# Low parts of every second weight tile of the second feed-forward product: from a VectorE subtraction to an adding DMA

## The chip, the cores and the metric

One Trainium2 chip; the kernel runs on one of its NeuronCores. The metric is the device time of one execution in microseconds (us), as the median of several runs. Engines are named as in the profile: PE (TensorE, its weight loads apart as PEld), DVE (VectorE), ACT (ScalarE), POOL (GpSimd) and SP (SyncE, which here only issues DMAs).

## What is computed

Two residual layers over 512 tokens of width 1024, and a final norm. Each layer has a token mixer (a state-space branch, a sparse attention, a retention, merged by gates) and a feed-forward part. The change lies in the feed-forward part, whose reference is:

```python
h2 = rms_norm(x, norm2_g[l])
x = x + jnp.square(jax.nn.relu(h2 @ w_ff1[l])) @ w_ff2[l]
```

`w_ff1` is 1024 x 4096 and `w_ff2` 4096 x 1024, in float32.

## The kernel before, in words

**Products in three passes.** Every large product keeps float32 accuracy by splitting both factors into a head (`wh`, `sqh`, ... of type float32r) and a low part (`wl`, `sql`, ...). `mm3` (L256) adds three matmuls into one PSUM bank: head by head, low part of the activation by the head of the weight, and head of the activation by the low part of the weight. So the low part of a weight tile is needed by one matmul in three.

**Weight tiles.** `wload` (L225) makes one tile of 128 partitions by up to 1024 floats (512 KB): SP issues a DMA from HBM into `raw`, ACT copies `raw` to the head `wh`, and DVE subtracts, `wl = raw - wh` (L233). Each of the three has three buffers, shared by all weight tiles of the kernel, those of `wload7` too. A buffer of `raw` is free for the next load when nobody has to read it any more; before, that is when the subtraction is done. A buffer of `wh` and `wl` is free when the last matmul on it is done.

**The feed-forward stage.** `layer` walks over 8 groups of 512 hidden features. For each group and each `part` (0, 1), it calls `ff1` for a piece of the next group, and then `ff2(e, part)` (L1194). `ff1` multiplies by a seven-product scheme: four tiles from `wload7` (128 x 896, DVE builds three of their blocks out of the others by additions in `raw`), 21 matmuls of 256 columns on each, into four PSUM banks named `f7` (the profile calls them `f`), and then DVE and ACT square and split the result (`zz`, `sqh`, `sql`). `ff2` calls `fm_blocks` (L261) for four blocks of 128 output features, two at a time: `b0` = 0 and `b0` = 2. Each pair needs one tile of `w_ff2`, 128 x 1024, with 24 matmuls of 512 columns on it, and DVE adds the two PSUM banks (`mm`) to the residual `xp`. So one `ff1` and one `ff2` are six weight tiles: four of 84 matmuls together, and two of 24 each. The last group of the second layer goes another way (256 columns at a time) and is not touched by the change. While layer 0 is in this stage, DVE, ACT and POOL also prepare the state-space tables of layer 1 (`s5_prep`).

**What sets the order.** Each engine runs its instructions in order. The order is found at build time by the framework's scheduler, which works on its own estimates; weight tiles are called under `high_priority` (look-ahead 3000), so that their copies and subtractions are pulled ahead as far as the buffers allow. All weight loads are in one line on SP.

Of the kernel before, what the change touches and what calls it, by code (L numbers as in the profile page):

```python
# [13 lines left out]
ALU = mybir.AluOpType  # L14

P = 128
SEQ = 512
# [76 lines left out]
def build(tc, x, positions, norm1_g, w_in, lam_re, lam_im, log_step, b_re, b_im, c_re, c_im, ssm_d,  # L94
# [26 lines left out]
    pe, ve, sc, gp, sy = (Ordered(e) for e in (nc.tensor, nc.vector, nc.scalar, nc.gpsimd, nc.sync))  # L121
    es = contextlib.ExitStack()
    with es:
# [4 lines left out]
        def f(t):  # L128
            return t.bitcast(F32)
# [9 lines left out]
        def spage(dtype=F32, name="tb"):  # L139
            return page(dtype, name, "tb")  # L140
# [13 lines left out]
        def copy(o, i, scale=1.0):  # L154
            sc.activation(o, i, AF.Copy, scale=scale)
# [66 lines left out]

        LOOK = 3000

        def wload(src, a, n, look=LOOK):  # L225
            with tc.high_priority(look):
                raw = pool.tile([P, 1024], F32, tag="raw", bufs=3, name="raw")
                h = pool.tile([P, 1024], F32R, tag="wh", bufs=3, name="wh")
                lo = pool.tile([P, 1024], F32R, tag="wl", bufs=3, name="wl")
                rv, hv, lv = (z[:, :a * n].rearrange("p (a n) -> p a n", a=a) for z in (raw, h, lo))  # L230
                sy.dma_start(out=rv, in_=src.rearrange("(k p) n -> p k n", p=P))
                copy(h[:, :a * n], raw[:, :a * n])
                ve.tensor_tensor(lo[:, :a * n], raw[:, :a * n], f(h[:, :a * n]), ALU.subtract)  # L233
            return hv, lv

        def wload7(src, look=LOOK):
# [17 lines left out]
        def mm3(ps, sh, sl, mh, ml, first, last, after=None):  # L254
            r = pe.matmul(ps, sh, mh, start=first, stop=False)
            if after is not None:  # L256
                tc.add_manual_dep(r.ins, after, order, reason="held back")
            pe.matmul(ps, sh, ml, start=False, stop=False)
            pe.matmul(ps, sl, mh, start=False, stop=last)

        def fm_blocks(w, c0, nblk, xh, xl, psf, n=SEQ, look=LOOK, after=None):  # L261
            kb = len(xh)
            step = 4 if kb == 2 else 2
            kp = min(kb, 4)
            for b0 in range(0, nblk, step):
                ps = [None] * step
                for k0 in range(0, kb, kp):
                    wh, wl = wload(w[k0 * P:(k0 + kp) * P, c0 + b0 * P:c0 + (b0 + step) * P], kp, step * P, look)
                    for j in range(step):
                        if k0 == 0:  # L270
                            ps[j] = psf()
                        cc = slice(j * P, (j + 1) * P)
                        for k in range(kp):
                            mm3(ps[j][:, :n], wh[:, k, cc], wl[:, k, cc], xh[k0 + k], xl[k0 + k], k0 + k == 0, k0 + k == kb - 1, after)
                        after = None
                for j in range(step):
                    yield b0 + j, ps[j]
# [419 lines left out]
        def s5_glu(l, gf, res):  # L697
            gh, gl = [], []
            for g in gf:
                h, lo = spage(F32R, "s5h"), spage(F32R, "s5l")  # L700
                copy(h, g)
                lo_of(lo, g, h)
                gh.append(h)
                gl.append(lo)
            wh, wl = wload(glu_w[l], 2, 256)
            for m in range(2):
                ps = mx_ps("glu")
                for k in range(2):
                    mm3(ps, wh[:, k, m * P:(m + 1) * P], wl[:, k, m * P:(m + 1) * P], gh[k], gl[k], k == 0, k == 1)
                th = spage(name="s5q")  # L710
                sc.activation(th, ps, AF.Tanh, scale=0.25, bias=glb2[:, 2 * l + m:2 * l + m + 1])
                stt(th, th, 1.0, gf[m], ALU.add, ALU.mult)
                h, lo = page(F32R, "yah"), page(F32R, "yal")
                copy(h, th, 0.25)
                stt(lo, th, 0.25, f(h), ALU.mult, ALU.subtract)
                res.append((h, lo))


        def tm_group(l, c0, n, nrm, psf):
            pss = [psf() for _ in range(NT)]  # L720
            for kk in range(0, KB, 2):
                wp = wload(w_in[l][kk * P:(kk + 2) * P, c0:c0 + n], 2, n)
                for k in range(kk, kk + 2):
                    wh, wl = wp[0][:, k - kk], wp[1][:, k - kk]
                    for t in range(NT):
                        c = slice(t * P, (t + 1) * P)
                        mm3(pss[t][:, :n], nrm.h[k][:, c], nrm.l[k][:, c], wh, wl, k == 0, k == KB - 1)
            return pss

        def tr4(blocks, psf=None):  # L730

            ps = (psf or mx_ps)("tr")
            for t, b in enumerate(blocks):
                w = b.shape[-1]
                pe.transpose(ps[:w, t * P:(t + 1) * P], b, ident)
            return ps
# [307 lines left out]
        def proj(w, y, psf):  # L1044
            return fm_blocks(w, 0, KB, [a for a, _ in y], [b for _, b in y], psf, look=50)

        def layer(l, nrm, o5):
# [7 lines left out]
            def gates(br, b0, b1, pages, after=None):  # L1055
                return {b0 + b: gate_tile(ps, rb, pages)
                        for b, ps in fm_blocks(w_in[l], C_GATE + br * DM + b0 * P, b1 - b0, nrm.h, nrm.l, mm_ps, look=50, after=after)}
# [6 lines left out]
            def fill():  # L1064
                for b, ps in fm_blocks(w_in[l], C_GATE, KB, nrm.h, nrm.l, mm_ps, look=50):
                    acc[b] = gate_tile(ps, rb)
                return gates(2, 0, 2, gpage)
# [126 lines left out]
            def ff2(e, part):  # L1194
                hs, ls = sq[e]
                w2 = w_ff2[l][e * 512:(e + 1) * 512]
                if e < NE - 1 or l + 1 < DEPTH:
                    for m, ps in fm_blocks(w2, 4 * part * P, 4, hs, ls, mm_ps):
                        m += 4 * part
                        ve.tensor_tensor(xp[m], xp[m], ps, ALU.add)  # L1200
                        if e == NE - 1:
                            n3.feed(m, g1[:, (l + 1) * KB + m:(l + 1) * KB + m + 1])
                    return
                if part:
                    return
                fg = []
                for hf in range(2):
                    z = spage(name="fg")
                    sy.dma_start(out=z, in_=fin_g[hf * 512:(hf + 1) * 512].partition_broadcast(P))
                    fg.append(z)  # L1210
                for th in range(2):
                    cc = slice(256 * th, 256 * th + 256)
                    for m, ps in fm_blocks(w2, 0, KB, [q[:, cc] for q in hs], [q[:, cc] for q in ls], mm_ps, 256):
                        ve.tensor_tensor(xp[m][:, cc], xp[m][:, cc], ps[:, :256], ALU.add)
                        n3.feed(m, None, None, cc)
                    finish(n3, th, fg)

            def finish(n3, th, fg):
                ts = range(2 * th, 2 * th + 2)
                ot = {}  # L1220
                for hf in range(2):
                    for t in ts:
                        ps = tr4([xp[4 * hf + m][:, t * P:(t + 1) * P] for m in range(4)])
                        ot[t, hf] = spage(name="ot")
                        ve.tensor_tensor(ot[t, hf], ps, fg[hf], ALU.mult)
                r, _ = n3.stats(False, ts)
                for q, (t, hf) in enumerate((t, hf) for hf in range(2) for t in ts):
                    z = ot[t, hf]
                    if q % 2 == 1:
                        copy(z, z, r[:, t:t + 1])  # L1230
                    else:
                        ve.tensor_scalar(z, z, r[:, t:t + 1], None, op0=ALU.mult)
                    (sy if q % 2 == 0 else sc).dma_start(out=out[0, t * P:(t + 1) * P, hf * 512:(hf + 1) * 512], in_=z)
# [5 lines left out]
            for e in range(NE):  # L1239
                for part in range(2):  # L1240
                    if e + 1 < NE:
                        ff1(2 * e + 2 + part)
                    ff2(e, part)
                if e:
                    next(steps, None)
# [6 lines left out]
        for m in range(KB):  # L1252
            if m == 4:
                glb2 = more_consts()
            ps = tr4([xt[m // 4, t][:, (m % 4) * P:(m % 4 + 1) * P] for t in range(NT)])
# [28 lines left out]
```

## Time and profile before

| | us |
|---|---|
| median of 3 runs | 1519.19 (1518.92 to 1520.07) |
| profiled execution | 1518.57 |
| its span, first to last instruction | 1516.8 |
| PE busy | 1468.6 (97%) |
| DVE busy | 1224.0 (81%) |
| ACT busy | 696.2 (46%) |
| POOL busy | 59.3 (4%) |
| feed-forward stage, layer 0 | about 450 to 790 of the span |
| feed-forward stage, layer 1 | about 1190 to 1500 |

The page gives busy times, the share of 40 slices of the span, the chain of work that ended last, the costliest groups of instructions and the DMA issues. PE's busy time includes pipelined matmuls, so two matmuls overlap in it; the distance from start to start says how fast they follow each other.

### The profile page before, as it was taken

What the parts mean: (1) busy time and instruction counts of PE and PEld (TensorE: products, weight loads), DVE (VectorE), ACT (ScalarE), POOL (GpSimd) and SP (SyncE); (2) the same over time, 40 slices, a digit from 0 to 9 for tenths busy, and PEclk for the clock granted to TensorE, in tenths of its full rate; (3) what the DMA queues carried; (4) which work ended last, traced back from release to release, by engine and by line L of the source; (5) the groups of instructions that cost most, each with busy time, mean ns of one, the idle gap of its engine ahead of it and who ended that gap; (6) DMA issues with size and microseconds to landing.
All of it is one profiled execution on the core that took longest, in us unless ns stands there. A gap on an engine that the chain in (4) does not pass through costs nothing.

```text
span 1516.8 us, 22081 instructions
## 1 busy us (share of the span) xinstructions
PE 1468.6 (97%) x8202; PEld 1288.4 (85%) x8202; DVE 1224.0 (81%) x2618; ACT 696.2 (46%) x1154; POOL 59.3 (4%) x131
## 2 busy tenths in 40 slices
PE   5999999999998999999999999999999999999997
PEld 5888988877887998889888889988778888998887
DVE  7876899985899878987775769998568888777876
ACT  5654653453534443344455743344445434343343
POOL 0211100000010000100001100000000000000000
PEclk9899999999999999999999999999999999999999
DMA  6221222323322333233342223322143323333343
GB/s 221 77 81 42 81 70 73 94 70 101 108 63 91 111 98 99 83 108 95 119 130 76 84 57 94 94 70 84 56 153 90 95 93 98 111 98 102 94 126 111
DMA packets 138993, 144.17 MB, mean 95 GB/s; under 512 B 11835, under 2 KB 131461, under 8 KB 138885
## 3 DMA queue, kind: packets, MB, share of 16 engines
q1 hardware_dynamic: 138132, 141.63, 31.0%
q8 instruction: 64, 1.05, 0.3%
q10 hardware_dynamic: 752, 1.12, 0.2%
q14 instruction: 45, 0.36, 0.1%
HBM read 136.44 MB, written 6.29 MB: 94 GB/s over the span
## 4 chain that ended last, share of the span: by engine, by line
PE 83%; DVE 10%; ACT 4%; issue 2%; DMA 1%; POOL 0%; SPq 0%; POOLq 0%; DVEq 0%; ACTq 0%
PE mm L110 58%; PE f L110 17%; DVE wl L110 2%; ACT u L110 1%; PE mx L110 1%; PE pv L110 1%; PE sp L110 1%; PE ry L110 1%; PE tr L110 1%; DVE zr L110 1%; DVE ang L110 1%; PE pt L110 1%; ACT s5f L110 1%; DVE x L110 1%; PE s5y L110 1%
## 5 line engine op out<-in xcount | busy, mean ns | idle before, releaser
L110 ACT ACTIVATE wh<-raw 128x1024 fp32r<-128x1024 f32 (+4 forms) x318 | 310.4, 978 | 528.6 <-PE mm L110 287.7
L110 DVE TENSOR_TENSOR wl<-raw,wh 128x1024 fp32r<-128x1024 f32 (+4 forms) x318 | 355.2, 1118 | 120.0 <-ACT wh L110 116.7
L110 PE MATMUL f<-xc,wh 128*128 128x256 f32 x1344 | 242.8, 281 | 0.0
L110 PE MATMUL mm<-sql,wh 128*128 128x512 f32 (+1 forms) x544 | 207.2, 382 | 1.3 <-DVE sql L110 1.2
L110 PE MATMUL mm<-sqh,wh 128*128 128x512 f32 (+1 forms) x544 | 207.0, 382 | 1.3 <-DVE fft L110 1.1
L110 PE MATMUL mm<-sqh,wl 128*128 128x512 f32 (+1 forms) x544 | 206.1, 381 | 0.0
L110 PEld LDWEIGHTS f<-xc,wh 128*128 128x128 f32 x1344 | 205.4, 188 | 0.0
L110 PE MATMUL f<-xc,wl 128*128 128x256 f32 x644 | 174.6, 281 | 1.3 <-DVE wl L110 1.3
L110 PE MATMUL mm<-xgh,wh 128*128 128x512 f32 x384 | 152.3, 397 | 0.0
L110 PE MATMUL mm<-xgh,wl 128*128 128x512 f32 x384 | 152.1, 397 | 0.0
L110 PE MATMUL mm<-xgl,wh 128*128 128x512 f32 x384 | 151.9, 396 | 0.0
L110 DVE TENSOR_TENSOR raw<-raw 128x256 f32<-128x256 f32 (+1 forms) x336 | 107.3, 330 | 30.0 <-DMA raw<-in_w_ff_dram 27.8
L110 PEld LDWEIGHTS mm<-sql,wh 128*128 128x128 f32 x544 | 102.3, 188 | 21.6 <-DVE sql L110 1.9
L110 PEld LDWEIGHTS mm<-sqh,wh 128*128 128x128 f32 x544 | 102.2, 188 | 21.7 <-issue 1.5
L110 PEld LDWEIGHTS f<-xc,wl 128*128 128x128 f32 x644 | 118.7, 188 | 1.9 <-DVE wl L110 1.5
L110 PEld LDWEIGHTS mm<-sqh,wl 128*128 128x128 f32 x544 | 102.4, 188 | 21.0
L110 PE MATMUL mm<-wl,xgh 128*128 128x384 f32 (+1 forms) x320 | 107.5, 338 | 1.7 <-DVE wl L110 1.7
L110 PE MATMUL mm<-wh,xgh 128*128 128x384 f32 (+1 forms) x320 | 103.5, 340 | 4.6 <-ACT z L110 2.8
L110 PE MATMUL mm<-wh,xgl 128*128 128x384 f32 (+1 forms) x320 | 104.5, 338 | 0.0
L110 DVE TENSOR_TENSOR x<-x,mm 128x512 f32<-128x512 f32 (+1 forms) x136 | 88.3, 650 | 12.9 <-PE mm L110 12.6
L110 PEld LDWEIGHTS mm<-xgh,wl 128*128 128x128 f32 x384 | 72.3, 188 | 16.1
L110 PEld LDWEIGHTS mm<-xgl,wh 128*128 128x128 f32 x384 | 72.3, 188 | 15.5
(383 smaller groups left out, 2676.9 us busy)
## 6 DMA issues: line engine op xcount, KB each, us to landing
raw<-in_w_ff_dram SPq DMA_DIRECT2D x76, 512.0 KB, 3.5
raw<-in_w_ff_dram SPq DMA_DIRECT2D x112, 256.0 KB, 2.8
raw<-in_w_in_dram SPq DMA_DIRECT2D x52, 512.0 KB, 3.6
raw<-in_w_in_dram SPq DMA_DIRECT2D x32, 384.0 KB, 3.3
raw<-in_w_out_dram SPq DMA_DIRECT2D x16, 512.0 KB, 3.4
xd<-x SPq DMA_DIRECT2D x16, 256.0 KB, 2.2
x<-xd SPq DMA_DIRECT2D x16, 256.0 KB, 5.6
raw<-in_w_proj_c_dram SPq DMA_DIRECT2D x8, 384.0 KB, 3.2
```

The costliest lines, as they stand in the source:

```text
L110: r = fn(*a, **k)
```

## The change

`wload` gets a flag `far`. With it, POOL writes the negated head into `wl`, and a DMA that POOL issues adds `raw` to it in place: `wl = -wh + raw`. `fm_blocks` sets the flag for every second step of its outer loop, and `ff2` asks for it. With four blocks in steps of two, that is the tile of `b0` = 0 in each call: 16 calls in layer 0 and 14 in layer 1, so 30 tiles.

```diff
-        def wload(src, a, n, look=LOOK):
+        def wload(src, a, n, look=LOOK, far=False):
...
                 copy(h[:, :a * n], raw[:, :a * n])
-                ve.tensor_tensor(lo[:, :a * n], raw[:, :a * n], f(h[:, :a * n]), ALU.subtract)
+                if far:
+                    gp.tensor_scalar(lo[:, :a * n], f(h[:, :a * n]), -1.0, None, op0=ALU.mult)
+                    gp.dma_start(out=lo[:, :a * n], in_=raw[:, :a * n], accum_op=ALU.add)
+                else:
+                    ve.tensor_tensor(lo[:, :a * n], raw[:, :a * n], f(h[:, :a * n]), ALU.subtract)
...
-        def fm_blocks(w, c0, nblk, xh, xl, psf, n=SEQ, look=LOOK, after=None):
+        def fm_blocks(w, c0, nblk, xh, xl, psf, n=SEQ, look=LOOK, after=None, far=False):
...
-                    wh, wl = wload(w[k0 * P:(k0 + kp) * P, c0 + b0 * P:c0 + (b0 + step) * P], kp, step * P, look)
+                    wh, wl = wload(w[k0 * P:(k0 + kp) * P, c0 + b0 * P:c0 + (b0 + step) * P], kp, step * P, look, far and b0 % (2 * step) == 0)
...
-                    for m, ps in fm_blocks(w2, 4 * part * P, 4, hs, ls, mm_ps):
+                    for m, ps in fm_blocks(w2, 4 * part * P, 4, hs, ls, mm_ps, far=True):
```

The scheduler answers with another order. PE, DVE and SP show it, at the same point of layer 1 (the fourth period of its feed-forward stage in the changed kernel).

PE, before: the first matmuls on the tile of `b0` = 0 (`wh_12027`, `wl_12028`), right behind the last ones of `ff1`. `sqh` and `sql` are the activations.

```order
L110 MATMUL f7_11885<-xc_11512,wl_11979 128x256
L110 MATMUL mm_12032<-sqh_11585,wh_12027 128x512
L110 MATMUL mm_12032<-sql_11586,wh_12027 128x512
L110 MATMUL mm_12032<-sqh_11585,wl_12028 128x512
L110 MATMUL mm_12032<-sqh_11592,wh_12027 128x512
```

PE, with the change, same point: the tile of `b0` = 0 is now `wh_12044`, `wl_12045`, that of `b0` = 2 `wh_12079`, `wl_12080`.

```order
L110 MATMUL mm_12050<-sqh_11601,wh_12044 128x512
L110 MATMUL mm_12050<-sql_11602,wh_12044 128x512
L110 MATMUL mm_12063<-sqh_11601,wh_12044 128x512
L110 MATMUL mm_12063<-sql_11602,wh_12044 128x512
L110 MATMUL mm_12084<-sqh_11601,wh_12079 128x512
L110 MATMUL mm_12084<-sql_11602,wh_12079 128x512
L110 MATMUL mm_12097<-sqh_11601,wh_12079 128x512
L110 MATMUL mm_12097<-sql_11602,wh_12079 128x512
L110 MATMUL mm_12084<-sqh_11601,wl_12080 128x512
```

Before, PE takes the low part with its third matmul on the tile. Now it does four matmuls on the head of the changed tile, then all 24 of the other tile, whose low part it takes after four.

PE, with the change, 19 matmuls further: the end of the tile of `b0` = 2, a piece of the next `ff1` (`wh_12117`, `wl_12118`), and the first use of the changed low part.

```order
L110 MATMUL mm_12097<-sqh_11684,wl_12080 128x512
L110 MATMUL f7_12112<-xq_11209,wh_12117 128x256
L110 MATMUL f7_12112<-xz_11210,wh_12117 128x256
L110 MATMUL f7_12112<-xq_11209,wl_12118 128x256
L110 MATMUL f7_12113<-xq_11209,wh_12117 128x256 x2
L110 MATMUL f7_12113<-xq_11209,wl_12118 128x256
L110 MATMUL f7_12115<-xq_11209,wh_12117 128x256
L110 MATMUL mm_12050<-sqh_11601,wl_12045 128x512
```

So the changed low part is first used after 4 + 24 matmuls of 512 columns and 7 of 256.

DVE, with the change, same point: the two last `wl` of `ff1`, and what follows them.

```order
L110 TENSOR_TENSOR wl_11966<-raw_11964,wh_11965 128x896
L110 TENSOR_TENSOR wl_11996<-raw_11994,wh_11995 128x896
L110 TENSOR_TENSOR raw_12116<-raw_12116 128x256
L110 TENSOR_TENSOR raw_12116<-raw_12116 128x128 x2
L110 TENSOR_TENSOR wl_12080<-raw_12078,wh_12079 128x1024
L110 TENSOR_TENSOR zz_12024<-f7_11901,zw_12025 128x2x256
```

Before, a subtraction for the tile of `b0` = 0 stood between the second and the third of these rows; it is gone. The first addition in `raw` for the tile after `wh_12117`, which stood ahead of the `zz` row, comes four rows behind it now.

SP, with the change, the loads from the tile of `b0` = 2 on, with what each waits for (DMAHW is a semaphore of a DMA that SP issued, DMASW of one that POOL issued):

```order
L110 DMA raw_12078<-in_w_ff2_dram 128x4x256 [waits DMAHW7_49,DVE_49]
L110 DMA raw_12116<-in_w_ff1_dram 128x2x256 [waits DMAHW0_49,DVE_49]
L110 DMA raw_12146<-in_w_ff1_dram 128x2x256 [waits DMAHW2_49,DVE_49]
L110 DMA raw_12176<-in_w_ff1_dram 128x2x256 [waits DMAHW3_49,DVE_49]
L110 DMA raw_12206<-in_w_ff1_dram 128x2x256 [waits DMAHW1_49,DMASW1_49]
```

The order of the loads is as before. The last of them, the fourth tile of the next `ff1`, gets the `raw` buffer of the changed tile, and waits for the adding DMA, where before it waited for DVE.

## Rows read from the trace of the kernel before

**Rows 1.** The page: busy time by engine, and the chain that ended last.

```profile
PE 1468.6 (97%) x8202; PEld 1288.4 (85%) x8202; DVE 1224.0 (81%) x2618; ACT 696.2 (46%) x1154; POOL 59.3 (4%) x131
...
PE 83%; DVE 10%; ACT 4%; issue 2%; DMA 1%; POOL 0%; SPq 0%; POOLq 0%; DVEq 0%; ACTq 0%
```

**Rows 2.** Chain of work, 1200 to 1300 us, merged: start, duration, what.

```profile
1207.04 9.93 PE f L110 x84
1216.97 11.15 PE mm L110 x48
```

**Rows 3.** Stretches: PE, PEld, DVE, ACT, POOL busy, granted clock, DMA share, GB/s.

```profile
455.00:480.00 25.00, 21.10 (x123) 17.57 (x123) 24.64 (x48) 13.10 (x19) 0.00 (x0) 1.00 0.20 64
628.00:650.00 22.00, 19.93 (x120) 17.20 (x119) 21.65 (x49) 5.36 (x6) 2.93 (x5) 1.00 0.14 41
1200.00:1250.00 50.00, 50.00 (x304) 44.47 (x303) 41.76 (x77) 21.36 (x28) 0.00 (x0) 1.00 0.32 100
```

**Rows 4.** PE's waits on DVE, 455 to 482 us, then 620 to 652 us.

```profile
PE f L110 <- DVE wl L110: 1.3, 1, 1.3
PE mm L110 <- DVE sql L110: 1.2, 1, 1.2
PE mm L110 <- DVE fft L110: 1.1, 1, 1.1
...
PE f L110 <- DVE wl L110: 1.2, 1, 1.2
```

**Rows 5.** DVE in order of time, the two tiles of one `ff2`.

```profile
1213.03 1.23 DVE L110 TENSOR_TENSOR wl<-raw,wh 128x1024 fp32r<-128x1024 f32 x1 [1.51 <-ACT wh L110]
1214.84 1.08 DVE L110 TENSOR_TENSOR raw<-raw 128x256 f32<-128x256 f32 x3 [0.58 <-DMA raw<-in_w_ff_dram]
1215.84 1.22 DVE L110 TENSOR_TENSOR wl<-raw,wh 128x1024 fp32r<-128x1024 f32 x1
```

**Rows 6.** ACT in order of time, the tile of `b0` = 0 there (start, duration, [idle before]).

```profile
1211.93 1.06 ACT L110 ACTIVATE wh<-raw 128x1024 fp32r<-128x1024 f32 x1 [1.55 <-PE f L110]
```

**Rows 7.** PE in order of time: first matmul on the tile of `b0` = 0.

```profile
1216.81 0.40 PE L110 MATMUL mm<-sqh,wh 128*128 128x512 f32 x1
```

**Rows 8.** Groups of POOL's instructions: busy, mean ns of one, idle before.

```profile
L110 POOL TENSOR_TENSOR r_rr<-r_rs,nhalf 128x4 f32<-128x4 f32 x8 | 8.7, 1088 | 189.3 <-DVE r_rs L110 189.3
L110 POOL MEMSET vi<- 128x512 f32 x4 | 2.1, 525 | 6.9 <-DVE cai L110 4.2 <-PE ctp L110 2.7
L110 POOL MEMSET zr<- 128x128 f32 x8 | 1.3, 202 | 0.1
L110 POOL COPY p_qi<-p_pi 128x16 f32<-128x16 f32 x4 | 0.9, 216 | 0.1
```

**Rows 9.** POOL in order of time, at four places, and DVE beside the fourth.

```profile
93.43 0.63 POOL L110 COPY pz<-pz 64x128 f32<-64x128 f32 x2 [29.42 <-ACT pz L110]
439.19 4.19 POOL L110 TENSOR_TENSOR st_r<-st_v,nhalf 128x4 f32<-128x4 f32 x1 [71.60 <-DVE st_v L110]
805.59 1.76 POOL L110 COPY u<-s5u 32x128 f32<-32x128 f32 x4 [13.74 <-DVE s5u L110]
864.84 2.71 POOL L110 COPY s5f<-s5g 32x128 f32<-32x128 f32 x4 [6.02 <-DVE s5g L110]
864.69 1.22 DVE L110 TENSOR_TENSOR wl<-raw,wh 128x1024 fp32r<-128x1024 f32 x1
```

**Rows 10.** The page: DMA issues, count, KB each, median us from issue to landing.

```profile
raw<-in_w_ff_dram SPq DMA_DIRECT2D x76, 512.0 KB, 3.5
raw<-in_w_ff_dram SPq DMA_DIRECT2D x112, 256.0 KB, 2.8
...
x<-xd SPq DMA_DIRECT2D x16, 256.0 KB, 5.6
```

**Rows 11.** Groups of DVE's instructions: busy, mean ns of one, idle before.

```profile
L110 DVE TENSOR_TENSOR sql<-zz,sqh 128x512 fp32r<-128x512 f32 x56 | 38.1, 684 | 0.0
L110 DVE TENSOR_TENSOR x<-x,mm 128x512 f32<-128x512 f32 x120 | 81.6, 681 | 11.6 <-PE mm L110 11.4
```

## The prediction

> **What bounds the kernel.** I read the page's busy times first, then the chain, then the stage that the change touches. PE is busy 97% of the span and holds 83% of the chain that ended last; DVE, which the change relieves, is busy 81% and holds 10% [rows 1]. Such averages say nothing of a stage, so the chain of the feed-forward stage comes next: in layer 1 it is PE alone, 84 matmuls of 256 columns in 9.93 us, then 48 of 512 columns in 11.15 us, over and over [rows 2]. That is 0.118 and 0.232 us for one, and 21.08 us for the six tiles of one `ff1` and one `ff2`. The stretches agree: from 1200 to 1250 us PE is busy all 50 us at a granted clock of 1.00 (2.4 GHz), DVE 41.76 and POOL not at all [rows 3]. No wait of PE's is listed there. Work taken from DVE can shorten nothing in such a stretch.
>
> Only in layer 0 does DVE hold up PE in this stage, in two stretches: 455 to 480 us, where DVE is busy 24.64 of 25 us, and 628 to 650 us, with 21.65 of 22 [rows 3]. PE lacks 3.9 us of the first and 2.1 of the second [rows 3], and the waits listed there are for the most part on DVE [rows 4]. **So 6.0 us, 0.4% of the time, is about all that this stage could give.**
>
> **What is removed.** 30 subtractions of 1.22 us on DVE [rows 5], 36.6 us of DVE time. Beside a PE that never waits they are worth nothing. Each of the two crowded stretches loses one subtraction ahead of PE's waits (a second one in the first stretch comes behind them), so there PE can gain 1.22 us each: 2.4 us at most.
>
> **What is added: a longer way to 30 low parts.** Before, in the period that I take as the pattern, ACT makes the head from 1211.93 to 1212.99 [rows 6], DVE subtracts until 1214.26 [rows 5], and PE begins the tile at 1216.81 [rows 7]. With the change the chain behind the head is POOL's multiplication and then the adding DMA. Their sum is not in the trace; I bound both.
>
> *POOL's multiplication, 1024 elements a partition.* POOL's fills take 202 ns for 128 elements and 525 for 512 [rows 8], 0.84 ns each. Copies read as well: 216 ns for 16 elements [rows 8], 0.315 us for 128 over 64 partitions and 0.44 over 32 [rows 9], which makes 0.9 to 2.0 ns each. From 216 ns, 1008 further elements give 1.1 to 2.2 us. I take 1.1, since the fills have the same slope as the lower copy; 2.2 goes into the range.
>
> *The adding DMA, 512 KB.* It moves as much as a weight load, 3.5 us from issue to landing, and reads its destination besides. From 256 KB to 512 KB a load grows by 0.7 us [rows 10], so 512 KB more would add 1.4: 4.9 us, which I take. The lower end is the load's 3.5. The upper end is the slowest copy of the page, 5.6 us for 256 KB [rows 10], twice: 11.2 us. I stay near the load, since the 5.6 us rows are eight loads issued in one go.
>
> So the chain takes 6.0 us, between 4.6 and 13.4.
>
> **What it may take.** By the order shown above, PE's first use of the changed low part now stands behind 4 + 24 matmuls of 512 columns and 7 of 256: 28 x 0.232 + 7 x 0.118 = 7.3 us after 1216.81, at 1224.1. The head is there at 1212.99. **The chain may take 11.1 us before PE waits; 6.0 leave 5.1 to spare**, in 28 of the 30 tiles (some have more). The cover is thus the other tile of the same `ff2` (5.6 us) and the 42 matmuls of `ff1` that run since the buffer came free (5.0 us). For each us beyond 11.1, PE would lose some 28 us.
>
> Three more waits come with it. (a) The adding DMA holds `raw` until 1212.99 + 6.0 = 1219.0, where DVE let it go at 1214.26. The load that waits for it, the fourth tile of the next `ff1`, is the last of its group on SP, so nothing of that group is queued behind it; it lands 2.8 us later [rows 10], 1221.8. On DVE the first addition for it stands ahead of the subtraction for the second tile of that `ff1`, whose low part PE needs at about 1230.6 (1224.1, then 20 matmuls of 512 columns and 16 of 256). Between lie three additions, 1.08 us together [rows 5], one `sql` and one `x`, 0.68 each [rows 11], and the subtraction, at most 1.22 [rows 5]: 3.7 us. This way, too, breaks only when the chain takes over 1230.6 - 3.7 - 2.8 - 1213.0 = 11.1 us. (b) The other tile of `ff2` now goes first: its low part is needed after 8 matmuls, at 1218.7, where DVE finishes it at 1217.06 [rows 5]. It had 5.8 us to spare and keeps 1.6. (c) The DMA engines are busy 0.32 of this stage, 6.8 us in a period [rows 3]; 4.9 more still leave 9.4.
>
> **A rule that speaks against it.** POOL and DVE get in each other's way: four copies on POOL that take 1.76 us elsewhere took 2.71 beside a subtraction with two inputs in SBUF, and a small operation that takes 1.09 us [rows 8] took 4.19 in the middle of a crowded DVE [rows 9]. The subtraction itself kept its 1.22 us. The Trainium skill ("SBUF — State Buffer", Who interferes with whom) has the rule: a DVE instruction with two SBUF inputs and a GpSimd instruction that reads SBUF lock each other out for a whole instruction, whoever comes first. The trace agrees as far as POOL's side goes; no row here shows DVE waiting. By the rule each multiplication could cost DVE its 1.1 us, which gives back most of the 36.6 us. In the pattern period DVE would be idle when the multiplication starts, as the subtraction that stood there is gone, and the additions that follow begin at 1214.84 [rows 5], after 1212.99 + 1.1 = 1214.1. There the rows give no collision. In the two crowded stretches of layer 0 they do: the multiplication can wait 3.1 us (4.19 less 1.09). Two changed tiles lie there with less room: 42 matmuls of 256 columns and 10, or 8, of 512 between the free buffer and the low part, 7.3 and 6.8 us, less 1.1 for the head, so 6.2 and 5.7 for a chain of 6.0 to 9.1. They can come up to 3 us late each, in stretches whose DVE work has become 1.2 us shorter. I set this against the gain of 2.4 us: nothing.
>
> For the adding DMA alone, the skill's page "DMA: Bandwidth & Descriptors" (Anatomy of one DMA) gives 2.0 us plus the bytes at 436 GB/s for a GpSimd DMA, by which 512 KB would take an estimated 3.2 us, or 4.4 when the second read is counted; the sum stays nothing.
>
> **The sum.** Profiled execution 1518.57, that is 1516.8 of span and 1.8 around it; 28 tiles at 0; the two crowded stretches at 0. The median of the runs is 0.6 above that execution. **I forecast no change, 1519.2 us.** What a measurement can tell from no change here is about 0.2%, 3 us.
>
> **The rivals.**
>
> *The chain takes over 11.1 us (slower).* It decides at a multiplication and DMA of 11.1 us together; the place is the first use of the low part in each `ff2`. At my upper bounds, 2.2 + 11.2 = 13.4 us, PE loses 2.3 us in 28 tiles: 64 us, 1583 us. At 12 us it is 25 us, 1544. For it: no row shows an accumulation in a DMA or one that POOL issues, and the transfer shares the engines with loads. Against: it would need 2.8 times what a load of the same size takes. Chance 0.28.
>
> *DVE comes late for the other tile, or layer 0's two tiles do (slower by little).* The 1.6 us of (b) are used up when the multiplication holds DVE until after 1216.4. A multiplication of 2.2 us ends at 1215.2, so it takes something like the 3.1 us wait in every period; at 0.5 us late in 28 tiles 14 us are lost, 1533 us. If only the two tiles of layer 0 are late by 3 us each, the time is 1525. Chance 0.12.
>
> *DVE's relief counts for more than its own time (faster).* If the new order closes the waits of both crowded stretches, up to 6.0 us go: 1513.2 us. With the 2.4 us of two subtractions alone it would stay under 0.2%. For it: those waits all have DVE behind them, directly or not. Against: the collisions above fall exactly there. Chance 0.08.
>
> That the change does not do what it says I leave out: the order shows 30 multiplications and 30 DMAs on POOL, and 30 subtractions fewer.
>
> **How the numbers follow.** No change has 0.52, the two slower cases 0.28 + 0.12 = 0.40, faster 0.08. The range goes from 1516.0, which leaves out most of the faster case, to 1580, almost the price of the chain at my upper bounds; below it may lie 0.06 and above it 0.09. The likeliest case alone lies between 1516.2 and 1522.2.
>
> **What would show it.** Right: PE's chain of layer 1 still alternates 9.93 and 11.15 us; POOL shows 30 multiplications of 1.1 to 2.2 us; the DMA issues have 30 of 512 KB from POOL that land in about 5 us; DVE's busy time is some 35 us lower. Wrong: PE waits on the DMA of `wl` in `ff2`, some 28 times; or on DVE for `wl` of the second tile; or the crowded stretches of layer 0 grow or close by more than 3 us. A landing time over 9 us would by itself make the forecast wrong.

## The result: 1 % slower, all of it lost in layer 0

| | before | after |
|---|---|---|
| median | 1519.06 us | 1534.10 us |
| ratio, 95% interval | | 1.0102 (1.0084 to 1.0119) |
| profiled execution / its span | 1518.57 / 1516.8 | 1534.17 / 1531.8 |
| feed-forward stage of layer 0 | 347.5 us | 363.0 us |
| feed-forward stage of layer 1 | 335.5 us | 335.8 us |

A stage is counted here from the first matmul of its norm (`statb`) to that of the next norm, or to the end. The span grew by 15.0 us, and layer 0's stage alone by 15.5. The mixers in between kept their times to 0.1 us. So the forecast of no change (1519.2) did not come; the time lies in the range.

The page of the kernel after, beside [rows 1] and [rows 8]: busy times, the chain by engine, groups of instructions (busy, mean ns of one, idle before), and a DMA issue (count, KB each, median us to landing).

```profile
PE 1473.8 (96%) x8202; PEld 1290.9 (84%) x8202; DVE 1189.3 (78%) x2588; ACT 694.8 (45%) x1154; POOL 173.9 (11%) x191
...
PE 80%; DVE 7%; DMA 5%; ACT 4%; issue 2%; POOL 1%; SPq 0%; POOLq 0%; DVEq 0%; ACTq 0%
...
L110 DVE TENSOR_TENSOR raw<-raw 128x256 f32<-128x256 f32 (+1 forms) x336 | 106.4, 331 | 132.9 <-DMA raw<-in_w_ff_dram 127.1
L110 POOL TENSOR_SCALAR wl<-wh 128x1024 fp32r<-128x1024 f32 x30 | 88.1, 2938 | 477.1 <-ACT wh L110 442.9
...
wl<-raw POOLq DMA_DIRECT2D x30, 512.0 KB, 5.2
```

DVE has lost 34.7 us of work, as foretold, and PE is no better for it. DMAs have come into the chain with 5%. POOL's multiplication takes 2.9 us on average, not 1.1.

**Layer 1.** The chain of waits, kernel after, in layer 1 (start, duration, what); it answers to [rows 2]:

```profile
1222.60 9.12 PE f L110 x77
1231.72 6.50 PE mm L110 x28
1238.22 0.83 PE f L110 x7
1239.05 4.65 PE mm L110 x20
1243.71 9.12 PE f L110 x77
```

It is PE alone, 21.1 us a period as before, only cut up by the new order. In that period POOL does this (start, duration; the idle time before it and what ended that stand at the end):

```profile
1227.89 2.76 POOL L110 TENSOR_SCALAR wl<-wh 128x1024 fp32r<-128x1024 f32 x1 [16.96 <-ACT wh L110]
1231.06 0.90 POOL L110 DMA_DIRECT2D wl<-raw  x1 [0.41 <-POOL wl L110]
```

ACT's head ends at 1227.79; the DMA lands 4.9 us after its issue (the DMA view of 1225 to 1240 us), at 1236.0. So the chain takes 8.2 us. PE starts the changed tile at 1231.72 and comes to its low part 28 + 7 matmuls later, at 1239.05: 3 us to spare.

**Layer 0.** The stretches of [rows 3] in the kernel after, and a short one behind the first wait (PE, PEld, DVE, ACT, POOL busy, granted clock, DMA share, GB/s):

```profile
455.00:480.00 25.00, 18.44 (x96) 15.32 (x95) 20.97 (x36) 9.92 (x15) 10.84 (x6) 0.93 0.29 74
628.00:650.00 22.00, 16.26 (x98) 14.85 (x97) 20.93 (x48) 8.13 (x16) 8.19 (x11) 0.84 0.32 84
...
468.00:472.00 4.00, 3.98 (x11) 3.17 (x12) 1.46 (x5) 0.63 (x2) 0.00 (x0) 0.58 0.24 66
```

PE now lacks 6.6 us of the first and 5.7 us of the second, against 3.9 and 2.1 before, and the granted clock, 1.00 before, is 0.93 and 0.84. PE in order of time in the first stretch:

```profile
461.01 0.47 PE L110 MATMUL mm<-sqh,wh 128*128 128x512 f32 x1 [1.17 <-DVE fft L110]
...
462.25 0.39 PE L110 MATMUL mm<-sqh,wl 128*128 128x512 f32 x1
468.02 0.79 PE L110 MATMUL mm<-sqh,wl 128*128 128x512 f32 x1 [5.39 <-DMA wl<-raw]
468.62 0.63 PE L110 MATMUL mm<-sqh,wh 128*128 128x512 f32 x1
469.04 0.63 PE L110 MATMUL mm<-sql,wh 128*128 128x512 f32 x1
```

PE waits 5.4 us for the first changed low part, and then runs for some 3 us at a pitch of 0.43 us instead of 0.23, at 1.2 instead of 2.4 GHz. What made the low part late stands on POOL, in the same stretch:

```profile
455.10 7.80 POOL L110 TENSOR_SCALAR wl<-wh 128x1024 fp32r<-128x1024 f32 x1 [12.41 <-ACT wh L110]
463.24 1.09 POOL L110 DMA_DIRECT2D wl<-raw  x1 [0.33 <-POOL wl L110]
464.01 0.87 POOL L110 MEMSET car<- 128x512 f32 x1
...
640.68 2.94 POOL L110 TENSOR_SCALAR wl<-wh 128x1024 fp32r<-128x1024 f32 x1 [1.92 <-ACT wh L110]
```

The multiplication that takes 2.76 us beside an idle DVE took 7.80 here, beside one without a gap. The last row is that of the second stretch: there it took 2.94 us, though DVE was busy for 2.90 of them, so a busy DVE does not always make it late. PE waited in the second stretch (620 to 660 us) 3.8 us for DVE's subtractions and 1.9 us for a head, and not for the adding DMA. The rest of the loss is in many small waits. I went through the starts of all of PE's matmuls in the stage and added up what lies over the plain pitch (0.232 us for 512 columns, 0.118 for 256), apart for matmuls at about twice the pitch (half clock) and for other gaps. Before: 8.0 us of gaps and 0.6 at half clock; after: 20.7 and 4.7. What remains of the stage is 338.8 and 337.6 us. **So the 15.5 us are 12.7 us of gaps and 4.1 us of half clock, less 1.2 us.** The same account for every kernel below is in the table behind the experiments.

### The profile page after: what moved, and what is told of

Its sections match the earlier page's. It is cut to its first block, busy times and chain, and to the rows that moved or that the text cites. A ratio compares the mean times of both kernels' runs of the same rounds, so it can differ in the third digit from the quotient of the medians.

```text
span 1531.8 us, 22189 instructions
## 1 busy us (share of the span) xinstructions
PE 1473.8 (96%) x8202; PEld 1290.9 (84%) x8202; DVE 1189.3 (78%) x2588; ACT 694.8 (45%) x1154; POOL 173.9 (11%) x191
## 4 chain that ended last, share of the span: by engine, by line
PE 80%; DVE 7%; DMA 5%; ACT 4%; issue 2%; POOL 1%; SPq 0%; POOLq 0%; DVEq 0%; ACTq 0%
PE mm L110 57%; PE f L110 14%; DMA raw<-in_w_ff_dram 3%; DVE wl L110 2%; ACT u L110 1%; PE mx L110 1%; DMA wl<-raw 1%; POOL wl L110 1%; PE pv L110 1%; PE sp L110 1%; PE ry L110 1%; DVE x L110 1%; PE tr L110 1%; PE s5y L110 1%; PE pt L110 1%
## 5 line engine op out<-in xcount | busy, mean ns | idle before, releaser
L110 DVE TENSOR_TENSOR wl<-raw,wh 128x896 fp32r<-128x896 f32 (+3 forms) x288 | 317.8, 1106 | 67.5 <-ACT wh L110 66.0
L110 PE MATMUL mm<-sqh,wl 128*128 128x512 f32 (+1 forms) x544 | 200.2, 385 | 6.6 <-DMA wl<-raw 5.4
L110 POOL TENSOR_SCALAR wl<-wh 128x1024 fp32r<-128x1024 f32 x30 | 88.1, 2938 | 477.1 <-ACT wh L110 442.9
L110 ACT ACTIVATE sqh<-zz 128x512 fp32r<-128x512 f32 x56 | 35.0, 625 | 132.3 <-DVE zz L110 132.3
```

The source lines that it names most:

```text
L110: r = fn(*a, **k)
```

## The experiments

The theory after this look: the loss arises in layer 0 alone, where DVE also prepares tables, and it has two causes. A1: the low part comes late (POOL's multiplication, then the DMA). A2: the adding DMA holds one of three load buffers `raw` for some 8 us behind the head, so that loads come late and DVE, which takes its work in order, lets PE wait. Rivals: each changed tile costs the same; the new order of the program costs it.

**E1, E2, E3, E5: which tiles.** The call of `fm_blocks` in `ff2`:

```diff
-  hs, ls, mm_ps, far=True)
+  hs, ls, mm_ps, far=l == 1)                                          # E1
+  hs, ls, mm_ps, far=l == 0)                                          # E2
+  hs, ls, mm_ps, far=(l, e, part) in ((0, 0, 0), (0, 4, 0)))          # E3
+  hs, ls, mm_ps, far=(l, e, part) not in ((0, 0, 0), (0, 4, 0)))      # E5
```

> The changed way is kept for the 14 tiles of layer 1 alone; the 16 tiles of layer 0 get their subtraction on VectorE back. Theory A (the loss arises in layer 0 alone, where VectorE also prepares the tables of the next layer): 1519.1 us, within 2 us of the kernel before, and PE's chain of layer 1 still alternates about 9.95 and 11.15 us. Rival B (every changed tile costs the same, 15.0 / 30 = 0.5 us): 14 x 0.5 = 7 us more than before, 1526. Rival C (the new order of the whole program costs it, wherever the tiles are): anything between 1519 and 1534, with stalls in layer 0 too.

Measured: 1519.2 us against 1519.3 of the kernel before, ratio 0.9998 (0.9990 to 1.0007). Its chain in layer 1 has the pieces shown above. 14 tiles cost nothing: Theory A.

> The changed way is kept for the 16 tiles of layer 0 alone. Theory A (all of the loss is layer 0's): 1534 us, within 3 us of the full change. Rival B (0.5 us a tile): 16 x 0.5 = 8 us more than before, 1527. Rival C (order): layer 0's stage changes by something else than in the full change, and the time is not predicted by either.

Measured: 1532.9 us, ratio 1.0086 (1.0073 to 1.0099). Layer 0's stage has 362.8 us, as with the full change. Rival B is out.

> The changed way is kept for two tiles alone, the first and the ninth of layer 0, which lie in the two stretches where VectorE has no idle time. Theory A in its narrow form (only the crowded stretches lose, by the late low part and by the backlog on VectorE behind it): about 5 to 9 us more than before, 1524 to 1528, with a wait of PE on the adding DMA of some 5 us in the first stretch. Theory A in its wide form (the lines of stalls between and behind those stretches count as well, as each adding DMA holds a load buffer): less, 1521 to 1525, and the other 14 tiles of layer 0 make up the rest. Rival B (0.5 us a tile): 1520.

Measured: 1523.0 us, ratio 1.0025 (1.0015 to 1.0036): the wide form of A. The wait on the adding DMA is there in full, and gaps stand nowhere but in the two crowded stretches and just behind them.

> The changed way for 28 tiles: the two tiles of the crowded stretches of layer 0 get their subtraction on VectorE back. If the losses add up (E3 showed 3.7 us for those two tiles alone, of 15.0): 15.0 - 3.7 = 11.3 us above before, 1530.5, without the wait of 5.4 us on the adding DMA in the first stretch. If the two tiles set off the other stalls of layer 0 (a backlog that drags on): 1519 to 1522.

Measured: 1525.2 us, ratio 1.0042 (1.0030 to 1.0055): between the two expectations. The 28 tiles cost 6.5 us without the two, the two cost 3.7 without the others, and together it is 15.0: some 5 us arise only when both sets are changed. That late low parts and held buffers meet there is the reading that fits; these runs do not show it.

**E4: the multiplication on ACT.**

```diff
-  gp.tensor_scalar(lo[:, :a * n], f(h[:, :a * n]), -1.0, None, op0=ALU.mult)
+  copy(lo[:, :a * n], f(h[:, :a * n]), -1.0)
   gp.dma_start(out=lo[:, :a * n], in_=raw[:, :a * n], accum_op=ALU.add)
```

> All 30 tiles; the negated head is written by ScalarE out of the loaded tile's head, the adding DMA stays on POOL. Theory A1 (the multiplication on POOL is what is late in the crowded stretches, since VectorE keeps POOL from its operands): the wait of PE on the adding DMA of 5.4 us in the first stretch goes, the chain behind the head becomes about 1.1 + 0.4 + 5.2 = 6.7 us everywhere, and the time falls to 1519 to 1525. Theory A2 (the adding DMA holds the load buffer too long, the multiplication matters little): the waits of VectorE on loads stay at about 130 us ahead of its additions in the load buffers, and the time stays between 1528 and 1534. Rival D (ScalarE becomes late with heads and squares, 30 x 1.06 = 32 us more on an engine that is busy 46%): above 1534, with more waits of PE on heads.

Measured: 1527.2 us, ratio 1.0044 (1.0031 to 1.0057), with single runs from 1522.9 to 1528.9. That lies between A1 and A2, and about half of the loss is gone. PE's waits in layer 0's stage (total, times, longest) show which half; the first row is that of the full change, the others are E4's:

```profile
PE f L110 <- DVE wl L110: 6.5, 6, 2.4
...
PE f L110 <- DVE wl L110: 5.1, 5, 2.3
PE mm L110 <- DVE fft L110: 2.2, 1, 2.2
PE mm L110 <- DMA wl<-raw: 1.7, 1, 1.7
```

The wait of 5.4 us on the adding DMA went; in its place stands one of 1.7, in the second crowded stretch. The waits on DVE's subtractions, 6.5 us in the full change, stayed at 5.1. E4's profile is that of its slowest run. A1 is a cause, and not the only one.

**E6, E7: the load buffer let go.** The adding DMA takes the weights from HBM again, in two halves; E7 has ACT's negation besides.

```diff
-  gp.dma_start(out=lo[:, :a * n], in_=raw[:, :a * n], accum_op=ALU.add)
+  sv = src.rearrange("(k p) n -> p k n", p=P)
+  for k in range(0, a, 2):
+      gp.dma_start(out=lv[:, k:k + 2], in_=sv[:, k:k + 2], accum_op=ALU.add)
```

> All 30 tiles; POOL's multiplication stays, but the adding DMA takes the weights from HBM a second time instead of from the load buffer (in two halves), so that the load buffer is free again as soon as ScalarE has made the head. Theory A2 (holding the load buffer is what costs in layer 0): VectorE's waits on loads fall from 127 us to about 30, as before the change, and only the late low part of the first tile is left: 1522 to 1526. Theory A1 (the late chain on POOL costs everywhere): no change or worse, since the chain gets longer by a second DMA issue: 1534 to 1545. If the engines of the DMAs are the limit (512 KB more from HBM in each period), VectorE's waits on loads stay above 100 us.

> Both suspected causes taken away: ScalarE writes the negated head, and the adding DMA reads HBM. If the late multiplication and the held load buffer are the two causes, the loss of 15.0 us goes, and VectorE's 36.6 us are left as relief of the crowded stretches: 1515 to 1520. If the new order is the cause: 1525 to 1535 as in the other kernels with 30 tiles.

Measured: E6 1545.6 us, ratio 1.0180 (1.0159 to 1.0200); E7 1560.1 us, ratio 1.0272 (1.0258 to 1.0287). Both runs failed as tests of A2, since the edit made the chain longer. POOL in order of time, E6, layer 1:

```profile
1212.72 2.79 POOL L110 TENSOR_SCALAR wl<-wh 128x1024 fp32r<-128x1024 f32 x1 [16.32 <-ACT wh L110]
1215.93 1.29 POOL L110 DMA_DIRECT2D wl<-in_w_ff_dram  x1 [0.41 <-POOL wl L110]
1220.61 1.20 POOL L110 DMA_DIRECT2D wl<-in_w_ff_dram  x1 [3.39 <-DVE zz L110]
```

POOL issues the second half only 3.4 us after it is done with the first, and it lands 4.3 us later: 12.3 us behind the head. PE then waits, in this stage too:

```profile
1225.10 0.50 PE L110 MATMUL mm<-sqh,wl 128*128 128x512 f32 x1 [0.16 <-DMA wl<-in_w_ff_dram]
```

Layer 1's stage grows by 6.4 us in E6 and 18.8 in E7, where the scheduler's order leaves PE some 9.8 us between head and second half (at the one place that I read) and the chain takes 10.2. So this confirms something else: layer 1 is free of loss only because the chain stays under some 11 to 12 us, as the prediction had it. The marker that I named for A2, DVE's waits on loads, turned out to be none: they were 93.0 us in E6, and 83.5 in E12, which has no adding DMA at all. A DVE that is relieved simply waits for the next load.

**E8, E9, E10: a fourth load buffer.** It takes the place of the held one; two temporary pages pay for it. E9 is E4 with this edit, E10 the kernel before with it.

```diff
-  raw = pool.tile([P, 1024], F32, tag="raw", bufs=3, name="raw")
+  raw = pool.tile([P, 1024], F32, tag="raw", bufs=4, name="raw")
...
-  "tb": 9
+  "tb": 7
```

> The full change with a fourth load buffer (and two pages fewer in the pool of temporary pages, which pays for it). Theory A2 (the held load buffer): a fourth buffer takes the place of the held one; VectorE's waits on loads fall to 30 to 60 us, and 1522 to 1527 if the two pages are not missed. Theory A1: unchanged, 1530 to 1535.

Measured: 1527.4 us, ratio 1.0054 (1.0041 to 1.0068). Of that 4.8 us are lost ahead of the stage, in layer 0's mixer (412.7 us against 407.9), where the two pages are missed; E10 loses 3.9 us there. Layer 0's feed-forward stage falls from 363.0 to 353.8 us; in the kernel before, the same buffer is worth 1.1 us of the stage (E10). PE's waits there:

```profile
PE mm L110 <- DMA wl<-raw: 5.4, 1, 5.4
PE f L110 <- DVE wl L110: 3.0, 1, 3.0
```

The late first tile is untouched, and `f`'s waits on DVE's subtractions went from 6 to 1. Between the crowded stretches PE has no gap left; from 480 to 620 us, kernel after, then E8 (columns as above):

```profile
480.00:620.00 140.00, 138.02 (x872) 123.57 (x871) 103.33 (x192) 57.25 (x75) 25.75 (x14) 1.00 0.46 123
```

```profile
480.00:620.00 140.00, 140.00 (x887) 126.38 (x886) 113.55 (x197) 57.82 (x76) 24.95 (x13) 1.00 0.46 124
```

The DMA engines are as busy (0.46) in both, so it is the buffer and not the traffic. A load of 256 KB takes 4.1 us to land in this stretch in the kernel after, 3.0 in E8 and 2.8 before. SP's queue shows loads that wait for the adding DMA in layer 0's stage, in the kernel after and then in E8; before, all but 0.5 us of its waits there were on DVE:

```profile
SPq L110 <- DMA wl<-raw: 45.4, 15, 6.9
...
SPq L110 <- DMA wl<-raw: 48.7, 16, 8.2
```

So the fourth buffer does not shorten this wait. What it takes away is PE's gaps behind it: the wait alone is no measure of the loss.

How a late load reaches PE is seen at the first of the small gaps. The adding DMA is issued at 490.13 and lands 5.8 us later; the load that waits for its buffer is issued at 495.90 and lands 4.7 us later. On DVE (kernel after, in order of time):

```profile
500.67 0.43 DVE L110 TENSOR_TENSOR raw<-raw 128x256 f32<-128x256 f32 x1 [2.14 <-DMA raw<-in_w_ff_dram]
...
501.66 0.69 DVE L110 TENSOR_TENSOR sql<-zz,sqh 128x512 fp32r<-128x512 f32 x1
...
503.27 1.08 DVE L110 TENSOR_TENSOR wl<-raw,wh 128x896 fp32r<-128x896 f32 x1
```

and on PE, which waits for that subtraction:

```profile
504.41 0.38 PE L110 MATMUL f<-xc,wl 128*128 128x256 f32 x1 [1.03 <-DVE wl L110]
```

> All 30 tiles, with both changes that helped alone: ScalarE writes the negated head (E4: 7.9 us above before) and a fourth load buffer stands behind the held one (E8: 8.7 us above before). If the late low part of the first tile and the held load buffer are the two causes and add up (15.0 less 7.1 less 6.3): 1518 to 1523, with no wait of PE on the adding DMA above 1 us and the lines of small stalls between the crowded stretches gone. If both took away the same part: 1525 to 1528. If a third cause is there (the new order, or the load of the DMA engines): 1524 or more, with stalls in other places.

Measured: 1524.4 us, ratio 1.0039 (1.0027 to 1.0052). The stage has 351.3 us; E10, with the same buffers and no changed tile, has 346.4. PE's waits in the stage:

```profile
PE mm L110 <- DMA wl<-raw: 6.6, 3, 3.1
PE f L110 <- DVE wl L110: 1.2, 2, 0.6
```

Against the expectation waits on the adding DMA remain, three of them, 6.6 us; those on DVE's subtractions are at E10's 1.2. So the two causes take part of their effect on the same time. Even with ACT's negation the chain is too long for the two crowded stretches and for the tile behind the second (the waits end at 467.8, 643.5 and 668.8 us). The time is also one that the expectation gave a third cause; the stalls that are left stand on the adding DMA, and no run excludes another order as part of it.

> The kernel before with the fourth load buffer and two temporary pages fewer, no tile changed. If the buffer only matters while an adding DMA holds one and the pages are not missed: 1517 to 1521. If the pages are missed, the time is above that, and this much of E8 and E9 is not the change's. If a fourth buffer helps by itself (loads land before the crowded stretches): 1513 to 1517.

Measured: 1521.9 us, ratio 1.0014 (1.0005 to 1.0023): the pages are missed (4 us), and the stage itself is 1.1 us shorter.

**E11: only where the relief counts.** The kernel before with E4's two lines under `far=(l, e) == (0, 0)`.

> The kernel before with only the first two tiles of layer 0's second product by the adding DMA, their negated head by ScalarE: the one stretch in which VectorE's relief can count. In E4 PE's stalls in that stretch were 3.0 us against 6.5 before. If that gain stands alone when the other 28 tiles are as before: 3 to 3.5 us off, 1515.5 to 1516.5. If E4's gain was paid back behind the stretch by the held load buffer: 1518 to 1521.

Measured: 1518.8 us against 1519.3, ratio 1.0000 (0.9992 to 1.0009). Gaps fell from 8.0 to 5.8 us, and matmuls at half clock rose from 0.6 to 3.3. PE in E11, at the head of the stretch:

```profile
463.72 0.47 PE L110 MATMUL mm<-sqh,wh 128*128 128x512 f32 x1 [2.19 <-DVE fft L110]
```

From 463 to 470 us, E11, then the kernel before (columns as above, the clock third from the end):

```profile
463.00:470.00 7.00, 6.28 (x20) 5.04 (x21) 7.00 (x15) 2.20 (x4) 0.00 (x0) 0.76 0.25 77
```

```profile
463.00:470.00 7.00, 4.55 (x17) 3.16 (x18) 7.00 (x18) 3.20 (x6) 0.00 (x0) 1.00 0.12 37
```

Before, two waits of 1.1 and 1.2 us and one of 0.2 stand in the stretch and the clock stays at 1.00; in E11 they are one wait of 2.2 us, and behind it the clock falls to 0.76, as it does in E4. The gain is given back, by the clock and not by a held buffer, as the expectation had it.

**E12: the relief without its price.** The loaded tile is left out of the 30 low parts, so this kernel lacks a part of the product.

```diff
-  gp.tensor_scalar(lo[:, :a * n], f(h[:, :a * n]), -1.0, None, op0=ALU.mult)
-  gp.dma_start(out=lo[:, :a * n], in_=raw[:, :a * n], accum_op=ALU.add)
+  copy(lo[:, :a * n], f(h[:, :a * n]), -1.0)
```

> The relief without its price: for the 30 tiles ScalarE writes the negated head into the low part's buffer and nothing is added to it, so that VectorE has its 30 subtractions less, but no adding DMA runs and no load buffer is held (the loaded tile is left out of these low parts). If the relief is worth what the prediction took: between 0 and 6.0 us below before, 1513 to 1519, with the stalls of layer 0's crowded stretches shorter. If the new order of the program costs something by itself, with no late low part and no held buffer: 1521 to 1528, as much as E9 had left.

Measured: 1515.7 us against 1519.7, ratio 0.9969 (0.9957 to 0.9981). Layer 0's stage has 343.8 us, 3.7 less than before; layer 1's is unchanged. In the crowded stretches PE lacks 2.1 and 0.5 us instead of 3.9 and 2.1:

```profile
455.00:480.00 25.00, 22.95 (x142) 19.60 (x141) 24.31 (x46) 13.03 (x18) 0.00 (x0) 1.00 0.26 77
628.00:650.00 22.00, 21.51 (x134) 19.09 (x133) 21.65 (x47) 7.99 (x10) 3.27 (x5) 1.00 0.20 61
```

So another order does not cost by itself, at least not this kernel's: with neither a late low part nor a held buffer the time falls.

**All stages together** (profiled executions, us; gaps and half clock are PE's in layer 0's stage, worked out as above):

| kernel | median | layer 0 | gaps | half clock | rest | layer 1 |
|---|---|---|---|---|---|---|
| before | 1519.1 | 347.5 | 8.0 | 0.6 | 338.8 | 335.5 |
| after | 1534.1 | 363.0 | 20.7 | 4.7 | 337.6 | 335.8 |
| E1 layer 1 only | 1519.2 | 349.9 | 9.0 | 2.0 | 338.9 | 336.0 |
| E2 layer 0 only | 1532.9 | 362.8 | 20.3 | 5.0 | 337.6 | 335.5 |
| E3 two tiles | 1523.0 | 353.0 | 11.7 | 2.5 | 338.8 | 335.5 |
| E5 all but two | 1525.2 | 354.1 | 13.3 | 3.1 | 337.8 | 336.4 |
| E4 ACT negates | 1527.2 | 356.1 | 14.2 | 4.0 | 337.9 | 336.9 |
| E6 from HBM | 1545.6 | 368.2 | 24.6 | 5.9 | 337.8 | 341.9 |
| E7 ACT, from HBM | 1560.1 | 372.0 | 26.9 | 7.3 | 337.8 | 354.3 |
| E8 four buffers | 1527.4 | 353.8 | 14.5 | 2.2 | 337.2 | 335.3 |
| E9 ACT, four buffers | 1524.4 | 351.3 | 10.1 | 4.3 | 337.0 | 334.4 |
| E10 before, four buffers | 1521.9 | 346.4 | 6.4 | 1.6 | 338.4 | 335.0 |
| E11 first two, ACT | 1518.8 | 348.0 | 5.8 | 3.3 | 339.0 | 335.5 |
| E12 relief alone | 1515.7 | 343.8 | 4.3 | 0.6 | 338.9 | 335.5 |

The rest is 337 to 339 us in all of them: whatever the order, PE's own work is the same, and the kernels differ by its gaps and its clock. Single executions of one kernel differ by up to 6 us (E4's), and the profiled ones of E4 and E8 lie 1.7 and 2.5 us above their medians, so differences of 1 to 3 us in the stage columns say little. The way that the full kernel pays for its relief is thus 363.0 - 343.8 = 19.2 us, for 3.7 us of relief. A fourth buffer takes 9.2 us of that away (1.1 of them it gives the kernel before as well), ACT's negation 6.9, both together 11.7. No version with all of the product in it beats the kernel before.

## Where the prediction was right and where it was wrong, step by step

**What bounds the kernel: right.** In layer 1 work taken from DVE is worth nothing, and the changed tiles cost nothing there (E1).

**The chain and its threshold: right where it was read.** The multiplication was mis-sized: 1.1 us taken, 2.2 as the upper bound, 2.76 measured beside an idle DVE. The fills and small copies of [rows 8, 9] were poor stand-ins for a pass that reads and writes 1024 elements. The DMA was taken at 4.9 us and measured at 4.9 in the pattern period, 5.2 in the median. With the issue on POOL and two gaps of 0.1 and 0.4 us ahead, the chain is 8.2 us, not 6.0; against 11.1 that made no difference, and E6 shows that the bound lies about there. The rival of the long chain, 1544 to 1583 us, did not come; E6 and E7 are that rival, made by hand.

**The other tile of (b): right, with less to spare.** DVE finishes its low part at 1231.74 + 1.22 = 1232.96; PE comes to it 8 matmuls after 1231.72, at 1233.58. That leaves 0.6 us, where 1.6 were forecast. From DVE's rows in layer 1:

```profile
1230.75 1.08 DVE L110 TENSOR_TENSOR raw<-raw 128x256 f32<-128x256 f32 x3 [4.49 <-DMA raw<-in_w_ff_dram]
1231.74 1.22 DVE L110 TENSOR_TENSOR wl<-raw,wh 128x1024 fp32r<-128x1024 f32 x1
```

**The step that failed is in the sum: "28 tiles at 0".** Step (a), the load buffer, was worked out in one period of layer 1 and carried to all tiles outside the two crowded stretches. 14 of these lie in layer 0, where DVE has tables to prepare as well. There a load that comes late leaves DVE idle at the head of its queue, and what stands behind it, PE's low parts among it, comes late too. The prediction had 6.0 us from the head to the end of the adding DMA and 2.8 for the load. At the first of the small gaps the rows give 8.9 (head at 486.97, landing at 495.89) and 4.7; in the pattern period of layer 1 it was 8.2 and 2.8. E5 has this without the two tiles: 6.5 us. E8 takes most of it away.

**The second one: "the two crowded stretches at 0".** The place was right, the size was not. The lock was priced at a wait of 3.1 us, and the low part at up to 3 us late; in the first stretch the multiplication took 7.80 us, 5.0 more than beside an idle DVE, and PE waited 5.4. In the second it took 2.94, and PE's waits there were on subtractions and a head. The loss was set against a relief of "2.4 us at most"; E12 shows 3.7 us of relief in the stage, under the bound of 6.0. That the waits of before were "for the most part on DVE" holds for both stretches together; from 620 to 652 us 1.6 of their 2.8 us were on ACT. And no term stood there for the clock: 4.1 us of the 15.5 are matmuls at half clock behind the new gaps.

**The rivals.** What came is the rival with 0.12, DVE late or layer 0's two tiles late. Its mechanism holds for the two tiles; its 1533 us were worked out for another form, 0.5 us in each of 28 tiles, and that they are near 1534.1 is chance. E1 rules that form out. For the two tiles alone it had 1525, and E3 gives 1523.0. The forecast had 0.52, and its own range, 1516.2 to 1522.2, missed. That the whole range, up to 1580, holds the time is luck: its upper part was there for the long chain, which did not come.

**The rule of the Trainium skill** ("SBUF — State Buffer", Who interferes with whom) was set against the change, and the trace bears it out on POOL's side, more than the prediction allowed for: 7.80 us against 2.76. The 5.0 us are longer than any one DVE instruction beside it (1.22 at most), so one lock for one instruction does not make them up. On DVE's side, of which no row of before showed anything, an operation with two SBUF inputs (`vr`, 64 x 256) took 1.17 us beside the multiplication at 640.68, where the 15 others of its form took 0.42. Another DVE operation stood beside POOL's issue and fills; DVE in order of time, kernel after, first crowded stretch:

```profile
457.50 0.43 DVE L110 TENSOR_SCALAR ang<-ang 128x512 f32<-128x512 f32 x1
...
463.70 2.85 DVE L110 TENSOR_SCALAR kk<-kk 128x512 f32<-128x512 f32 x1
```

The same form takes 0.43 us elsewhere, and 2.85 from 463.70 on, while POOL issues the DMA and runs its fills. In E6, where the fills come later, it took 0.71 beside the issue alone. The same section of the Trainium skill names `tensor_scalar` among the DVE operations whose modes can take the shared port, so that the one that comes second waits. The trace agrees; that it was the port, and not something else on POOL, no run here tells apart.

**What stays open.** How much of the loss is the multiplication's wait and how much its plain 2.76 us was not separated: E4 takes both away at once. E9's last waits on the adding DMA were not chased further. Each experiment also gives the scheduler another program, so that a part of each difference may be its order; E12 shows only that one such order does not cost. And why the multiplication took 7.80 us in one crowded stretch and 2.94 in the other stays open.

## What to carry to other kernels

A margin that is read in one period holds for that stage; before a cost is put at nothing for all tiles, read it again in the stage whose neighbour engine is full. Moving a step to a slower engine also moves the moment at which its input buffer comes free: with three buffers for a line of loads, one held some 7 us longer (8.2 us behind the head instead of 1.3) was worth about 8 us here, and a fourth took that away, at the price of two temporary pages. And relief for an engine that is not the bound is worth what its waits are worth: here 3.7 us out of 34.7 us of work.

## What the hardware did that I had not expected

- POOL's multiplication of 128 x 1024 elements took 2.76 us in the clear, 2.7 ns an element, against 0.84 for its fills [rows 8], and 7.80 us beside a DVE without gaps in one place, 2.94 in another.
- One wait of PE of 2.2 us was followed by a granted clock of 0.76 over the next 7 us, where two waits of 1.1 and 1.2 us and one of 0.2 had left it at 1.00 (E11 and before); behind the wait of 5.4 us it was 0.58 over 4 us. Fewer gaps in all can thus cost as much time as more.
- Two adding DMAs from HBM of 256 KB each did not follow each other at once on POOL: 3.4 us of idle time lay between their issues (E6). Why, the rows do not tell.
